# The first norm's squares on one engine, and the MLP's first three products side by side

## The chip, the core and the metric

The program runs on one core of a Trainium2 chip. Its engines work side by side and wait for one another by semaphores: TensorE (PE) multiplies, VectorE (DVE), ScalarE (ACT) and GpSimd (POOL) do elementwise work, and SyncE (SP) hands transfers to the DMA queues. The metric is the device time of one execution in microseconds, as the median of the runs shown.

## The reference

Two transformer blocks in a row, in float32, on 512 tokens of 1024 features. The change touches the first block alone.

```
def rmsnorm(x, g):
    y = x * rsqrt(mean(x * x, axis=-1) + EPS) * g
def first_block(x, ...):
    h = rmsnorm(x, ln1)
    z = h @ w_in                      # split into a pooling, a gated-linear and a forgetting attention mixer
    mix = concat(y_pool, y_gla, y_fox)
    x = x + mix @ w_o
    h = rmsnorm(x, ln2)
    gate, up = split(h @ w_gu)        # 2 x 2816 columns
    x = x + (silu(gate) * up) @ w_down
```

## The kernel before

The activations lie transposed: `x[k]`, for k from 0 to 7, holds features 128k to 128k+127 on the partitions and the 512 tokens along the free axis. Every matrix is split into a high and a low half, so that a product over one row tile k takes three matmuls of 128x512 on TensorE: high weight by high activation (`wh`, `hh`), high by low (`wh`, `hl`), low by high (`wl`, `hh`). A product over all eight row tiles is 24 matmuls into one PSUM bank (`dense`). Banks with the tag `mm` are three, taken in turn.

A weight tile (`weight`) comes by one transfer into `wr` (two buffers), ScalarE makes `wh` of it (line 188) and VectorE or GpSimd makes `wl` (line 189, three buffers of each). The engine for `wl` alternates with the count of tiles. A buffer is free when its last reader has ended.

A norm does not stand before the product that uses it. The activations are scaled by the gain alone and multiplied, and the scale of each token, R = 1/sqrt(mean square), is applied when a product is taken out of PSUM. R itself takes a chain (`rstd`): the squares of the eight row tiles are added up in one tile `ss`; four small matmuls with a column of ones sum `ss` over the partitions (`col_sum`, the rows `tr<-ones,ss`); ScalarE takes the root (`col`), VectorE the reciprocal and its two parts (`part`); eight matmuls spread the result over all partitions (`spread`, rows `tr<-identr,part`); ScalarE copies it to `R`.

The order on TensorE is that in which the code calls it. The other engines' order is set by the tile framework's scheduler when the program is built, and SyncE sends transfers in a fixed order too, each as soon as its buffer is free.

The first norm, in `block1`: for each x[k], as its transfer lands, ScalarE makes `hh` (line 494) and VectorE `hl` (line 495). The four odd squares and their sum are made on GpSimd (lines 502 and 504), the four even ones on ScalarE and added on VectorE (`square_into`, lines 294 and 298), and line 508 adds the two sums. On TensorE, a first small product (`psg`) and, from row tile 3 on, the product `gq` run behind the arriving tiles; then `gk` follows, whose first 15 matmuls stand ahead of `col_sum`.

The MLP's entry: the output projection `w_o` ends with m = 7; for each m VectorE adds the product to x[m] (line 556), ScalarE makes `hh` and VectorE `hl` (lines 192 and 193), and the square goes to `ss`. Then `mlp` multiplies: product 0 (gate of tile 0) over all eight row tiles, product 1 (up of tile 0) with the chain of R inside it, then products 2 and 3 (tile 1), and so on. A gate product is taken out by line 860 (`g<-mm,R`) and an up product by line 864 (`u<-mm,R`).

Of the kernel before, what the change touches and what calls it, by code (L numbers as in the profile page):

```python
# [16 lines left out]
OP = mybir.AluOpType  # L17
# [3 lines left out]
P = 128  # L21
T = 512
D = 1024
KD = D // P
# [60 lines left out]
class Body:  # L85
# [388 lines left out]
    def block1(self, ctx, raw):  # L474
        nc, A, x = self.nc, self.A, self.x
        mp = self.pool(ctx, "mix")
        mix = [tuple(mp.tile([P, T], F32R, name=f"m{c}{k}") for c in "hl") for k in range(4)]
        b = lambda dt=F32: mp.tile([P, T], dt, tag="b", name="b", bufs=NB)

        wg = self.wp.tile([P, 1024], F32R, tag="wh", name="wh", bufs=3)  # L480
        wg3, raw3 = wg.rearrange("p (k m) -> p k m", m=P), raw[:, :512].rearrange("p (k m) -> p k m", m=64)
        self.split(wg3[:, :, :64], wg3[:, :, 64:], raw3)
        rq = self.wp.tile([P, 1024], F32, tag="wr", name="wr", bufs=WR)
        wq = [self.wp.tile([P, 1024], F32R, tag=t, name=t, bufs=3) for t in ("wh", "wl")]
        h = self.acts()
        sums = [self.sums(), self.sums()]
        for k in range(KD):
            for n, at in enumerate((XA, XB)):
                if k == at:
                    cols = slice(n * 512, n * 512 + 512)  # L490
                    nc.sync.dma_start(rq[:, cols], A["w1s"][T1["gq"]][:, cols])
                    self.split(*(w[:, cols] for w in (*wq, rq)))
            nc.sync.dma_start(x[k], A["xT"][k * P:(k + 1) * P, :])
            last = nc.scalar.activation(h[k][0], x[k], AF.Identity, scale=self.gain("ln1", k))
            nc.vector.scalar_tensor_tensor(h[k][1], x[k], self.gain("ln1", k), h[k][0].bitcast(F32),  # L495
                                           op0=OP.mult, op1=OP.subtract)
        self.ident = self.const(self.gp, "ident", [P, P])
        self.identr = self.gp.tile([P, P], F32R, name="identr")
        nc.scalar.activation(self.identr, self.ident, AF.Copy)
        for k in range(1, KD, 2):  # L500
            sq = sums[1] if k == 1 else self.tmp()
            nc.gpsimd.tensor_tensor(sq, x[k], x[k], op=OP.mult)
            if k > 1:
                nc.gpsimd.tensor_tensor(sums[1], sums[1], sq, op=OP.add)
        for k in range(0, KD, 2):
            with self.tc.issue_after(getattr(last, "ins", last)):
                self.square_into(sums[0], x[k], k == 0, eng=nc.vector)
        nc.vector.tensor_tensor(sums[0], sums[0], sums[1], op=OP.add)
        self.identb = self.const(mp, "identb", [P, P], BF16)
        self.causalb = self.const(mp, "causalb", [P, P], BF16)  # L510
        psg = self.bank("mm")
        gen = self.dense(wq, h)
        for k in range(KD):
            for half in (True, False) if k == KD - 1 else (False, True):
                if half:
                    self.mm(psg[:64], wg3[:, k, :64], h[k][1], False, False)
                else:
                    self.mm(psg, wg3[:, k, :], h[k][0], k == 0, k == KD - 1)
            if k >= XL:
                next(gen)  # L520
        psq = self.all(gen)
        gen = self.dense(self.slab("w1s", T1["gk"]), h)
        for _ in range(XS):
            next(gen)
        r = self.rstd(sums[:1], D)
        next(r)
        next(gen)
        next(gen)
        R, Rc = self.all(r)
        psk = self.all(gen)  # L530
        fd = self.dp.tile([8, T], F32, name="fd")
        V = [[], []]
        proj = self.fox_proj(h, R, b)
        with ExitStack() as c:
            self.gla_phase(c, h, R, Rc, mix, mp, b, fd, psg, (psq, psk), V, proj)
        self.share = 1
        with ExitStack() as c:
            xp = self.pool(c, "mix2")
            mix += [tuple(xp.tile([P, T], F32R, name=f"m{c}{k}") for c in "hl") for k in range(4, KD)]
            self.fox_phase(mp, b, mix, V, fd, proj, self.half_zero(xp))  # L540
            self.share = 2
            h2 = self.acts()
            ssum = self.sums()
            for m in range(KD):
                self.all(self.w_o(mix, m, 1))
                self.split_scaled(h2[m][0], h2[m][1], x[m], self.gain("ln2", m))
                self.square_into(ssum, x[m], m == 0, eng=nc.vector if m == KD - 1 else nc.gpsimd)
            self.last = [ssum]
        self.h = h2
# [236 lines left out]
    def fox_phase(self, mp, b, mix, V, fd, proj, klo):  # L786
# [26 lines left out]
        self.attention(begin, after, PFOX, 860, res=RESF, masked=True, norm=NFOX)  # L813
        self.flush()

    def mlp(self, ctx):
        nc, A, x = self.nc, self.A, self.x
        fp = self.pool(ctx, "ff")
        wd = self.pool(ctx, "wd")
        act = [tuple(fp.tile([P, T], F32R, name=f"f{c}{k}") for c in "hl") for k in range(FH)]  # L820
        lng = fp.tile([P, KD], F32, name="lng")
        o, o2 = GAINS["ln_f"][0], GAINS["norm_g"][0]
        nc.vector.tensor_tensor(lng, self.gains[:, o:o + KD], self.gains[:, o2:o2 + KD], op=OP.mult)
        ft = lambda tag: fp.tile([P, T], F32, tag=tag, name=tag, bufs=2)
        self.res = self.dp.tile([T, D], F32, name="res")

        def down(m, half):
            raw = wd.tile([P, FH * P], F32, tag="wd", name="wd", bufs=2)
            nc.sync.dma_start(raw, A["w1d"][half * KD + m])
            hi, lo = (wd.tile([P, FH * P], F32R, tag=t, name=t, bufs=2) for t in ("wdh", "wdl"))  # L830
            self.split(hi, lo, raw)
            return hi, lo

        def turn(m):

            s, o = ft("g"), ft("u")
            nc.scalar.activation(s, x[m], AF.Identity, scale=self.gain("ln_f", m))
            yield
            tr = self.bank("tr")
            for t in range(NT):  # L840
                self.tp(tr[:, t * P:(t + 1) * P], s[:, t * P:(t + 1) * P])
            nc.scalar.activation(o, tr, AF.Copy)
            nc.sync.dma_start(self.res[:, m * P:(m + 1) * P].rearrange("(t p) c -> p t c", p=P),
                              o.rearrange("p (t c) -> p t c", c=P))

        turns = []
        for half in range(2):
            for k in range(FH):
                m = half * FH + k
                ps = self.all(self.dense(self.slab("w1gu", 2 * m), self.h))  # L850
                gen = self.dense(self.slab("w1gu", 2 * m + 1), self.h)
                if m == 0:
                    r = self.rstd(self.last, D)
                    next(gen)
                    next(r)
                    for _ in range(3):
                        next(gen)
                    R = self.all(r)[0]
                g = ft("g")
                nc.vector.tensor_tensor(g, ps, R, op=OP.mult)  # L860
                nc.scalar.activation(g, g, AF.Silu)
                ps = self.all(gen)
                u = ft("u")
                nc.vector.tensor_tensor(u, ps, R, op=OP.mult)  # L864
                nc.vector.tensor_tensor(u, u, g, op=OP.mult)
                self.split(act[k][0], act[k][1], u)
            for m in range(KD):
                ps = self.all(self.dense(down(m, half), act, kt=FH))
                nc.vector.tensor_tensor(x[m], ps, x[m], op=OP.add)  # L869
                if half == 1:  # L870
                    if m == 0:
                        h = self.acts()
                        s1, s2 = self.sums(), self.sums()
                    self.split_scaled(h[m][0], h[m][1], x[m], lng[:, m:m + 1])
                    eng = nc.vector if m == KD - 1 else nc.gpsimd
                    self.square_into(s1, x[m], m == 0, eng=eng)
                    self.square_into(s2, x[m], m == 0, scale=self.gain("ln_f", m), eng=eng)
                    for g in turns:
                        self.all(g)
                    turns = [turn(m)]  # L880
                    next(turns[0])
        self.s1, self.s2 = [s1], [s2]
        self.h, self.turns = h, turns
# [584 lines left out]
```

## Time and profile before

| what | value |
|---|---|
| runs (us) | 1092.42, 1092.99, 1090.87; median 1092.42 |
| the profiled execution | 1092.89 us, of which the span of the records is 1090.3 us |
| granted TensorE clock, mean over the span | 0.985 of full |
| busy over the span | PE 97%, weight loads 80%, DVE 62%, ACT 50%, POOL 35% |
| chain that ended last, by engine | PE 75%, DVE 17%, ACT 3%, DMA 2%, issue 2% |

Times in rows are microseconds from the start of the span. A row with a count xN covers N instructions in a row, and its busy time is theirs together. A bracket at the end of a row is the engine's idle time ahead of it and what ended that. Neighbouring matmuls overlap in the records, so the pace of TensorE is read from the distance of their starts.

### The profile page before, as it was taken

The numbers are of one execution on the slowest core, as the hardware profiler recorded it, in microseconds if no ns is written. First come the engines' busy times: TensorE is split into PE (matmuls) and PEld (weight loads), VectorE is DVE, ScalarE is ACT, GpSimd is POOL, SyncE is SP. The second block draws the span as 40 slices with busy tenths as digits, with TensorE's granted clock in tenths as the row PEclk, the third lists the DMA queues.
The fourth block names the chain that finished last, engine by engine and source line by source line (L and its number), as shares of the span: only waits on it lengthen the run. The fifth ranks groups of instructions, "written<-read, shape, count | busy, mean of one in ns | idle before, by whom it ended". The sixth has DMA issues, their size and how long they took to land.

```text
span 1090.3 us, 14058 instructions
## 1 busy us (share of the span) xinstructions
PE 1053.8 (97%) x5264; PEld 871.0 (80%) x5264; DVE 675.2 (62%) x1137; ACT 543.2 (50%) x950; POOL 377.6 (35%) x221
## 2 busy tenths in 40 slices
PE   8999999998999999999999998989899999999997
PEld 4888877787888888888888787768787898888786
DVE  7654488885454432445444268899996566888652
ACT  5653578654232221223235465655655566678233
POOL 5233322133232300223123254433334346654454
PEclk9999999998999999999999999899999999999999
DMA  6322132252323323232323144232222323335842
GB/s 202 102 78 78 56 101 67 69 183 72 102 95 98 96 81 106 87 114 80 106 85 118 29 131 151 70 106 90 89 87 97 110 67 121 112 87 175 281 152 77
DMA packets 41690, 114.81 MB, mean 105 GB/s; under 512 B 4952, under 2 KB 9448, under 8 KB 41624
## 3 DMA queue, kind: packets, MB, share of 16 engines
q1 hardware_dynamic: 38536, 107.62, 30.6%
q10 hardware_dynamic: 2448, 4.22, 1.0%
q0 software_dynamic: 640, 2.10, 0.5%
q8 instruction: 41, 0.67, 0.2%
q14 instruction: 25, 0.20, 0.1%
HBM read 103.40 MB, written 13.14 MB: 107 GB/s over the span
## 4 chain that ended last, share of the span: by engine, by line
PE 75%; DVE 17%; ACT 3%; DMA 2%; issue 2%; SPq 0%; DVEq 0%; ACTq 0%
PE mm L151 64%; PE sc L151 4%; PE pv L151 3%; PE tr L151 2%; DVE score L1005 2%; PE tr L158 2%; DVE m L1004 2%; DVE kst L189 1%; DVE pl L387 1%; DMA wr<-in_w2uq_r 1%; DVE hl L193 1%; DVE b L311 1%; DVE qk L189 1%; DVE b L374 1%; DVE s L369 1%
## 5 line engine op out<-in xcount | busy, mean ns | idle before, releaser
L189 POOL TENSOR_TENSOR wl<-wr,wh 128x1024 fp32r<-128x1024 f32 (+2 forms) x107 | 263.3, 2461 | 560.9 <-ACT wh L188 547.9
L151 PE MATMUL mm<-hh,wh 128*128 128x512 f32 (+2 forms) x808 | 327.0, 405 | 2.4 <-DVE z L1076 1.6
L151 PE MATMUL mm<-hl,wh 128*128 128x512 f32 (+3 forms) x808 | 318.1, 394 | 5.9 <-DVE hl L495 3.5
L151 PE MATMUL mm<-hh,wl 128*128 128x512 f32 (+1 forms) x800 | 314.8, 394 | 0.0
L188 ACT ACTIVATE wh<-wr 128x1024 fp32r<-128x1024 f32 (+2 forms) x142 | 146.8, 1034 | 225.7 <-PE mm L151 186.4
L151 PEld LDWEIGHTS mm<-hl,wh 128*128 128x128 f32 (+2 forms) x808 | 153.5, 190 | 36.7 <-DVE hl L495 6.2
L151 PEld LDWEIGHTS mm<-hh,wh 128*128 128x128 f32 (+1 forms) x808 | 154.1, 191 | 34.5 <-DVE z L1076 2.0
L151 PEld LDWEIGHTS mm<-hh,wl 128*128 128x128 f32 (+1 forms) x800 | 151.5, 189 | 32.8
L151 PE MATMUL mm<-fh,wdh 128*128 128x512 f32 x176 | 70.1, 398 | 0.0
L151 PE MATMUL mm<-fl,wdh 128*128 128x512 f32 x176 | 69.6, 395 | 0.0
L151 PE MATMUL mm<-fh,wdl 128*128 128x512 f32 x176 | 69.6, 395 | 0.0
L864 DVE TENSOR_TENSOR u<-mm,R 128x512 f32<-128x512 f32 x22 | 15.2, 692 | 72.2 <-PE mm L151 72.2
L188 ACT ACTIVATE wdh<-wd 128x1408 fp32r<-128x1408 f32 x16 | 22.1, 1381 | 74.4 <-PE mm L151 70.5
L869 DVE TENSOR_TENSOR x<-mm,x 128x512 f32<-128x512 f32 x16 | 11.1, 692 | 74.2 <-PE mm L151 74.2
L189 DVE TENSOR_TENSOR fl<-u,fh 128x512 fp32r<-128x512 f32 x22 | 45.0, 2044 | 15.4 <-ACT fh L188 15.4
L387 DVE TENSOR_TENSOR pl<-tr,ph 128x128 fp32r<-128x128 f32 (+1 forms) x96 | 46.0, 484 | 11.2 <-ACT ph L386 10.2
L298 POOL TENSOR_TENSOR ss<-ss,t 128x512 f32<-128x512 f32 x21 | 30.8, 1479 | 51.9 <-ACT t L297 51.9
L371 ACT ACTIVATE s<-s,m 128x128 f32<-128x128 f32 (+1 forms) x64 | 35.8, 559 | 25.3 <-DVE m L369 24.9
L189 DVE TENSOR_TENSOR wl<-wr,wh 128x1024 fp32r<-128x1024 f32 (+1 forms) x34 | 42.4, 1248 | 8.0 <-ACT wh L188 7.8
L151 PE MATMUL mm<-wh,hh 128*128 128x256 f32 x160 | 46.5, 290 | 0.0
L151 PE MATMUL mm<-wl,hh 128*128 128x256 f32 x160 | 45.3, 283 | 0.0
L151 PE MATMUL mm<-wh,hl 128*128 128x256 f32 x160 | 45.2, 283 | 0.0
(345 smaller groups left out, 2022.9 us busy)
## 6 DMA issues: line engine op xcount, KB each, us to landing
wr<-in_w1gu SPq DMA_DIRECT2D x44, 512.0 KB, 3.5
wr<-in_w2s SPq DMA_DIRECT2D x39, 512.0 KB, 3.5
wd<-in_w1d SPq DMA_DIRECT2D x16, 704.0 KB, 4.3
wr<-in_w1s SPq DMA_DIRECT2D x15, 512.0 KB, 3.5
wr<-in_w1o SPq DMA_DIRECT2D x8, 512.0 KB, 3.5
wr<-in_w2o SPq DMA_DIRECT2D x8, 512.0 KB, 3.8
shear<-gd SPq DMA_DIRECT2D x1, 2560.0 KB
x<-in_xT SPq DMA_DIRECT2D x8, 256.0 KB, 5.8
```

The lines of the kernel that those rows point to most:

```text
L151: self.nc.tensor.matmul(out, l, r, start=start, stop=stop)
L158: self.nc.tensor.transpose(out, src, self.ident if ident is None else ident)
L188: self.nc.scalar.activation(hi, src, AF.Copy)
L189: (eng or self.nc.vector).tensor_tensor(lo, src, hi.bitcast(F32), op=OP.subtract)
L193: self.nc.vector.scalar_tensor_tensor(lo, src, scale, hi.bitcast(F32), op0=OP.mult, op1=OP.subtract)
L298: (eng or nc.gpsimd).tensor_tensor(ssum, ssum, sq, op=OP.add)
L371: nc.scalar.activation(s[:, :n], s[:, :n], AF.Exp, scale=-1.0, bias=m[:, 0:1], accum_out=m[:, 1:2])
L387: nc.vector.tensor_tensor(lo, trv, hi.bitcast(F32), op=OP.subtract)
L864: nc.vector.tensor_tensor(u, ps, R, op=OP.mult)
L869: nc.vector.tensor_tensor(x[m], ps, x[m], op=OP.add)
L1004: nc.vector.max(out=m8, in_=s)
L1005: nc.vector.match_replace(s, m8, s, -3.4e38)
```

## The change

In `block1`, all eight squares are made on ScalarE and seven are added on VectorE; GpSimd has no part in them, and there is one sum tile instead of two. In `mlp`, the first three products are started side by side in three banks: row tiles 0 to 5 of products 0, 1 and 2, then `col_sum`, then row tiles 6 and 7 of products 0 and 1, then `spread`, then row tiles 6 and 7 of product 2. The number of matmuls stays.

```diff
-        sums = [self.sums(), self.sums()]
+        ssum = self.sums()
...
-        for k in range(1, KD, 2):
-            sq = sums[1] if k == 1 else self.tmp()
-            nc.gpsimd.tensor_tensor(sq, x[k], x[k], op=OP.mult)
-            if k > 1:
-                nc.gpsimd.tensor_tensor(sums[1], sums[1], sq, op=OP.add)
-        for k in range(0, KD, 2):
+        for k in range(KD):
             with self.tc.issue_after(getattr(last, "ins", last)):
-                self.square_into(sums[0], x[k], k == 0, eng=nc.vector)
-        nc.vector.tensor_tensor(sums[0], sums[0], sums[1], op=OP.add)
+                self.square_into(ssum, x[k], k == 0, eng=nc.vector)
...
-        r = self.rstd(sums[:1], D)
+        r = self.rstd([ssum], D)
...
+    def entry(self):
+
+        n, late = 3, KD - 2
+        w = [self.weight(self.A["w1gu"][i]) for i in range(n)]
+        self.first = [self.bank("mm") for _ in range(n)]
+
+        def part(i, ks):
+            for k in ks:
+                (hi, lo), (ah, al), c = w[i], self.h[k], slice(k * P, (k + 1) * P)
+                self.mm(self.first[i], hi[:, c], ah, k == 0, False)
+                self.mm(self.first[i], hi[:, c], al, False, False)
+                self.mm(self.first[i], lo[:, c], ah, False, k == KD - 1)
+
+        r = self.rstd(self.last, D)
+        for i in range(n):
+            part(i, range(late))
+        next(r)
+        part(0, range(late, KD))
+        part(1, range(late, KD))
+        self.R2 = self.all(r)[0]
+        part(2, range(late, KD))
...
-                ps = self.all(self.dense(self.slab("w1gu", 2 * m), self.h))
-                gen = self.dense(self.slab("w1gu", 2 * m + 1), self.h)
                 if m == 0:
-                    r = self.rstd(self.last, D)
-                    next(gen)
-                    next(r)
-                    for _ in range(3):
-                        next(gen)
-                    R = self.all(r)[0]
+                    self.entry()
+                ps = self.first.pop(0) if self.first else self.all(self.dense(self.slab("w1gu", 2 * m), self.h))
+                gen = None if self.first else self.dense(self.slab("w1gu", 2 * m + 1), self.h)
```

The scheduler's order on VectorE at the first norm, from the last `hl` on, before (`ss` is the sum, `t` a square, the first `wl` that of `gk`, the second that of the second `gv` tile, `b` the small product taken from PSUM):

```order
L495 SCALAR_TENSOR_TENSOR hl7_150<-x7_117,gains_82,hh7_149 128x512
L298 TENSOR_TENSOR ss_151<-ss_151,t_198 128x512
L189 TENSOR_TENSOR wl_257<-wr_254,wh_256 128x1024
L298 TENSOR_TENSOR ss_151<-ss_151,t_201 128x512
L587 TENSOR_TENSOR b_339<-mm_212,t_340 64x512
L298 TENSOR_TENSOR ss_151<-ss_151,t_204 128x512
L508 TENSOR_TENSOR ss_151<-ss_151,ss_152 128x512
L189 TENSOR_TENSOR wl_370<-wr_367,wh_369 128x1024
L262 RECIPROCAL col_281<-col_281 128x4
```

And now:

```order
L495 SCALAR_TENSOR_TENSOR hl7_150<-x7_117,gains_82,hh7_149 128x512
L298 TENSOR_TENSOR ss_151<-ss_151,t_187 128x512
L298 TENSOR_TENSOR ss_151<-ss_151,t_190 128x512
L298 TENSOR_TENSOR ss_151<-ss_151,t_193 128x512
L189 TENSOR_TENSOR wl_257<-wr_254,wh_256 128x1024
L298 TENSOR_TENSOR ss_151<-ss_151,t_196 128x512
L298 TENSOR_TENSOR ss_151<-ss_151,t_199 128x512
L298 TENSOR_TENSOR ss_151<-ss_151,t_202 128x512
L298 TENSOR_TENSOR ss_151<-ss_151,t_205 128x512
L581 TENSOR_TENSOR b_339<-mm_212,t_340 64x512
L189 TENSOR_TENSOR wl_370<-wr_367,wh_369 128x1024
L262 RECIPROCAL col_281<-col_281 128x4
```

Seven adds to `ss` stand there instead of three, and the add of line 508 is gone (later lines are numbered six lower in the changed file). On ScalarE, at the same place, from the first square on, the order is now this (`wh_256` is `gk`, `wh_363` the first `gv` tile, `wh_369` the second):

```order
L294 ACTIVATE ss_151<-x0_110 128x512
L297 ACTIVATE t_187<-x1_111 128x512
L297 ACTIVATE t_190<-x2_112 128x512
L499 ACTIVATE identr_184<-c_ident_182 128x128
L297 ACTIVATE t_193<-x3_113 128x512
L188 ACTIVATE wh_256<-wr_254 128x1024
L297 ACTIVATE t_196<-x4_114 128x512
L297 ACTIVATE t_199<-x5_115 128x512
L297 ACTIVATE t_202<-x6_116 128x512
L188 ACTIVATE wh_363<-wr_361 128x1024
L297 ACTIVATE t_205<-x7_117 128x512
L580 ACTIVATE t_340<-mm_212 64x512
```

Before, only x2, x4 and x6 had a `t` there, and the first `gv` tile stood behind all of them; now the last square stands behind it. On TensorE at the MLP's entry the piece that carries the sum is the turn from the first to the last row tiles, which is now (`mm_2581`, `mm_2582`, `mm_2583` are products 0, 1 and 2):

```order
L151 MATMUL mm_2583<-hh5_2349,wh_2577 128x512
L151 MATMUL mm_2583<-hl5_2350,wh_2577 128x512
L151 MATMUL mm_2583<-hh5_2349,wl_2578 128x512
L151 MATMUL tr_2638<-ones_84,ss_2355 128x1 x4
L151 MATMUL mm_2581<-hh6_2351,wh_2565 128x512
L151 MATMUL mm_2581<-hl6_2352,wh_2565 128x512
L151 MATMUL mm_2581<-hh6_2351,wl_2566 128x512
L151 MATMUL mm_2581<-hh7_2353,wh_2565 128x512
L151 MATMUL mm_2581<-hl7_2354,wh_2565 128x512
L151 MATMUL mm_2581<-hh7_2353,wl_2566 128x512
```

Before, the matmuls of `hh6` and `hl6` in product 0 stood right behind those of `hl5` in the same product, with no others between. On ScalarE the `wh` of the fourth tile stood ahead of the root `col`; now the fourth and the fifth stand between `col` and `R`. On VectorE the `wl` of the fourth tile moved from ahead of the reciprocal to behind `part`. The order of transfers on SyncE is the same, and GpSimd has lost the seven instructions of the first norm and nothing else.

## Rows read from the trace of the kernel before

**Rows 1.** Whom TensorE waited for, whole span: total, times, longest.
```profile
PE mm L151 <- DVE hl L495: 3.5, 4, 2.1
PE mm L151 <- DVE hl L193: 2.3, 2, 2.2
```

**Rows 2.** Timeline of TensorE from 6 to 27 us: start, busy, instruction.
```profile
12.14 0.45 PE L151 MATMUL mm<-hl,wh 128*64 128x512 f32 x1 [2.11 <-DVE hl L495]
...
18.41 0.44 PE L151 MATMUL mm<-hl,wh 128*64 128x512 f32 x1 [0.33 <-DVE hl L495]
...
25.99 0.95 PE L151 MATMUL tr<-ones,ss 128*128 128x1 f32 x8
```

**Rows 3.** Timeline of VectorE from 0 to 60 us.
```profile
8.21 0.75 DVE L495 SCALAR_TENSOR_TENSOR hl<-x,gains,hh 128x512 fp32r<-128x512 f32 x1 [0.62 <-ACT hh L494]
...
10.33 3.20 DVE L495 SCALAR_TENSOR_TENSOR hl<-x,gains,hh 128x512 fp32r<-128x512 f32 x2
...
14.90 4.12 DVE L495 SCALAR_TENSOR_TENSOR hl<-x,gains,hh 128x512 fp32r<-128x512 f32 x3
...
19.54 1.21 DVE L189 TENSOR_TENSOR wl<-wr,wh 128x1024 fp32r<-128x1024 f32 x1
...
22.71 2.71 DVE L508 TENSOR_TENSOR ss<-ss 128x512 f32<-128x512 f32 x1
```

**Rows 4.** Timeline of GpSimd from 0 to 60 us.
```profile
14.39 3.41 POOL L504 TENSOR_TENSOR ss<-ss,t 128x512 f32<-128x512 f32 x2
22.32 2.54 POOL L189 TENSOR_TENSOR wl<-wr,wh 128x1024 fp32r<-128x1024 f32 x1 [4.52 <-ACT wh L188]
```

**Rows 5.** Timeline of ScalarE from 0 to 60 us.
```profile
10.79 2.09 ACT L494 ACTIVATE hh<-x,gains 128x512 fp32r<-128x512 f32 x3
12.79 0.61 ACT L294 ACTIVATE ss<-x 128x512 f32<-128x512 f32 x1
...
24.19 1.06 ACT L188 ACTIVATE wh<-wr 128x1024 fp32r<-128x1024 f32 x1 [1.95 <-DMA wr<-in_w1gv]
```

**Rows 6.** Timeline of SyncE's queue from 0 to 60 us.
```profile
15.00 6.11 SPq L197 DMA_DIRECT2D wr<-in_w1gv  x2
```

**Rows 7.** Chain that ended last, by line: 18 to 146, then 263 to 640 us.
```profile
by line: PE mm L151 79.4%; PE tr L151 7.1%; PE sc L151 6.8%; PE pv L151 5.0%; DVE hl L495 1.3%; PE tr L158 1.2%; DVE b L369 0.3%; issue 0.1%; DVEq L369 0.0%
by line: PE mm L151 98.3%; PE tr L158 1.0%; PE tr L151 0.8%
```

**Rows 8.** Timeline of TensorE from 245 to 278 us.
```profile
246.29 0.39 PE L151 MATMUL mm<-hh,wh 128*128 128x512 f32 x1
...
254.95 0.50 PE L151 MATMUL mm<-hl,wh 128*128 128x512 f32 x1 [2.16 <-DVE hl L193]
...
256.87 1.70 PE L151 MATMUL tr<-ones,ss 128*128 128x1 f32 x8
...
262.36 1.00 PE L151 MATMUL tr<-identr,part 128*128 128x128 f32 x8
...
266.00 0.39 PE L151 MATMUL mm<-hh,wh 128*128 128x512 f32 x1
...
276.88 0.39 PE L151 MATMUL mm<-hh,wh 128*128 128x512 f32 x1
```

**Rows 9.** Busy time by stretch: length, PE, PEld, DVE, ACT, POOL, granted clock, DMA.
```profile
258.00:260.00 2.00, 2.00 (x7) 1.71 (x8) 0.51 (x3) 0.26 (x1) 0.00 (x0) 0.50 0.49 164
```

**Rows 10.** Timeline of VectorE from 225 to 300 us.
```profile
252.28 2.62 DVE L193 SCALAR_TENSOR_TENSOR hl<-x,gains,hh 128x512 fp32r<-128x512 f32 x1 [0.79 <-ACT hh L192]
254.82 0.68 DVE L298 TENSOR_TENSOR ss<-ss,t 128x512 f32<-128x512 f32 x1
...
264.02 0.69 DVE L860 TENSOR_TENSOR g<-mm,R 128x512 f32<-128x512 f32 x1 [4.54 <-ACT R L280]
```

**Rows 11.** Timeline of GpSimd from 220 to 300 us.
```profile
252.00 2.35 POOL L189 TENSOR_TENSOR wl<-wr,wh 128x1024 fp32r<-128x1024 f32 x1
```

**Rows 12.** Timeline of ScalarE from 215 to 290 us.
```profile
263.39 0.60 ACT L280 ACTIVATE R<-tr 128x512 f32<-128x512 f32 x1 [4.52 <-PE tr L151]
```

More of the change, by code (lines that the diff above doesn't have):

```diff
@@ L849, in mlp @@
                 m = half * FH + k
-                ps = self.all(self.dense(self.slab("w1gu", 2 * m), self.h))
-                gen = self.dense(self.slab("w1gu", 2 * m + 1), self.h)
                 if m == 0:
-                    r = self.rstd(self.last, D)
-                    next(gen)
-                    next(r)
-                    for _ in range(3):
-                        next(gen)
-                    R = self.all(r)[0]
+                    self.entry()
+                ps = self.first.pop(0) if self.first else self.all(self.dense(self.slab("w1gu", 2 * m), self.h))
+                gen = None if self.first else self.dense(self.slab("w1gu", 2 * m + 1), self.h)
                 g = ft("g")
-                nc.vector.tensor_tensor(g, ps, R, op=OP.mult)
+                nc.vector.tensor_tensor(g, ps, self.R2, op=OP.mult)
                 nc.scalar.activation(g, g, AF.Silu)
-                ps = self.all(gen)
+                ps = self.first.pop(0) if gen is None else self.all(gen)
                 u = ft("u")
-                nc.vector.tensor_tensor(u, ps, R, op=OP.mult)
+                nc.vector.tensor_tensor(u, ps, self.R2, op=OP.mult)
                 nc.vector.tensor_tensor(u, u, g, op=OP.mult)
```

## The prediction

> **What bounds the kernel now.** I read the list of TensorE's waits first, then the chain that ended last by stretch, then the timelines of each engine at the two places of the change, with the granted clock beside them. TensorE is the engine that matters. From 18 to 146 us and from 263 to 640 us nearly every step of the chain is its own work [rows 7], so a microsecond taken from it ahead of these stretches should come out at the end. Two entries in its list of waits are the low halves of the two norms: 3.5 us for `hl` of line 495 and 2.3 us for `hl` of line 193 [rows 1].
>
> At the first norm VectorE is late because of GpSimd. An `hl` that runs alone takes 0.75 us; two of them together then take 3.20 and three take 4.12, 1.4 to 1.6 us each [rows 3], while GpSimd makes its squares and sums, the last of which end at 14.39 + 3.41 = 17.80 us [rows 4]. ScalarE has all its `hh` done at 10.79 + 2.09 = 12.88 us [rows 5], but the last `hl` ends at 14.90 + 4.12 = 19.02 us, six microseconds later. TensorE stands for 2.11 us ahead of 12.14 us, and still waits for an `hl` at 18.41 us [rows 2].
>
> At the MLP's entry the last `hl` is held up too: it takes 2.62 us from 252.28 us, and ends 0.55 us behind the 2.35 us of GpSimd from 252.00 us [rows 10, 11]. Product 0 needs it straight away, so TensorE waits 2.16 us [rows 8]. After that wait the granted clock is 0.50 of full, the lower level of 1.2 GHz, for the stretch from 258 to 260 us [rows 9]. So the wait is paid once as idleness and once more as slow matmuls.
>
> **The entry's price, worked out.** Product 0 starts at 246.29 us and product 4 at 276.88 us [rows 8]: 30.59 us for four products, one `col_sum` and one `spread`. At full clock 48 matmuls go from 266.00 to 276.88 us, 0.2267 us each [rows 8]. Four products are 96 matmuls, 21.76 us; `col_sum` at full clock is 0.95 us [rows 2] and `spread` 1.00 us [rows 8]. That is 23.71 us if nothing waits, **6.9 us less** than now.
>
> Does anything wait in the new order? The first 54 matmuls use only row tiles 0 to 5 and fill 246.29 to 258.53 us. `ss` is done at 254.82 + 0.68 = 255.50 us and the last `hl` at 254.90 us [rows 10], ahead of `col_sum` at 258.53 us and of their own use from about 259.5 us. Of the weights, product 2's `wl` is the tight one: it ends at 252.00 + 2.35 = 254.35 us on GpSimd [rows 11], and is first read by the 39th matmul, at 246.29 + 38 x 0.2267 = 254.90 us. It is 0.55 us to spare, the smallest margin I find. With no wait, nothing asks for the lower clock.
>
> What is late next is product 3. Its bank is that of product 0, which `g<-mm,R` must take out first. Now, from the start of `spread` at 262.36 us to the end of that multiply at 264.02 + 0.69 = 264.71 us are 2.35 us, with the copy to R at 263.39 us between [rows 8, 10, 12]. In the new order TensorE has `spread` (1.00) and six matmuls of product 2 (1.36) to do in that time, 2.36 us: they match, and I put 0.1 us for the wait. The weights of product 3 start later than now, since product 0 keeps its `wh` buffer until its last row tiles end, at 258.53 + 0.95 + 1.36 = 260.84 us. Then come 1.06 us of `wh` [rows 5] and 1.21 us of `wl` [rows 3], to 263.1 us, ahead of 264.6 us. The fifth `wh` now stands ahead of the copy to R on ScalarE. It needs product 1's buffer, free at 262.2 us, so it ends near 263.3 us, when `spread` ends too. That hides it; without this cover each microsecond of it would delay R and product 3 by as much. The entry's term is **-6.8 us**. Its bounds: -6.9, and +0 if the same waits come back elsewhere.
>
> **The first norm's price.** Without GpSimd, an `hl` takes 0.75 us [rows 3], and the last follows the last `hh` at 12.88 us: some 13.7 us instead of 19.0. The third `hl` waits for half a `wl` (I take 0.6 us, half of 1.21 [rows 3]) and ends near 8.96 + 0.6 + 0.75 = 10.3 us instead of 12.1. From there 48 matmuls stand ahead of `col_sum` (33 to the end of `gq`, 15 of `gk`): 10.9 us at full clock, so TensorE would come to `col_sum` at 21.2 us. Now it is there at 25.99 us [rows 2]. The upper bound of this term is thus 4.8 us.
>
> But `ss` must be ready. ScalarE has four more squares, 4 x 0.61 = 2.4 us [rows 5], and the last stands behind the `wh` of the first `gv` tile. Counted from 12.79 us: four squares, the small `identr` (0.3, an estimate from its quarter size), one `wh`, three squares, one `wh`. With starts 0.52 to 0.61 us apart, that `wh` ends at 18.7 to 19.5 us and the last square at 19.2 to 20.1. The tile's transfer is handed over at 15.00 us at the latest [rows 6]. The next tile's hand-over ends at 15.00 + 6.11 = 21.11 us, and its `wh` waits for the landing and starts at 24.19 us [rows 5, 6], about 3.4 us from one to the other. So the first lands by 18.4 us, and earlier if its buffer, released by VectorE's faster half `wl`, lets it go earlier.
>
> When that `wh` ends, GpSimd takes the tile's `wl`, 2.54 us [rows 4], to 21.2 or 22.0 us, and the last add falls in it. Beside the same kind of `wl` today, an add that started at 22.71 us took 2.71 us and ended at 25.42, 0.56 us after GpSimd's 22.32 + 2.54 = 24.86 us [rows 3, 4]. So I let the last add end 0.56 us after GpSimd, at 21.8 to 22.6 us, and `col_sum` with it: 3.4 to 4.1 us sooner than now. Behind the add, VectorE still has `b` and a `wl` of 1.21 us [rows 3] ahead of the reciprocal, as before. The root is there about a microsecond after `col_sum`, so the parts can come 0.2 us late for `spread`. My value is **-3.7 us**, between -4.8 and 0.
>
> Here the Trainium skill has a rule, in "SBUF — State Buffer", section "SBUF: two separate sides": a VectorE instruction with two SBUF inputs and a GpSimd instruction exclude each other, whichever starts first holds the shared ports for its whole length, and the other stands. By it the last add ends behind the `wl`, and the sum is as above. If the two only slowed each other down, as the 1.4 to 1.6 us per `hl` [rows 3] could also be read, the add would end by 21.5 us, and the term would be up to -4.8 us. The add that ends 0.56 us after GpSimd [rows 3, 4] and the `hl` that ends 0.55 us after it [rows 10, 11] speak for the rule.
>
> **What is free.** The seven instructions that GpSimd loses lie off the chain, apart from what they do to VectorE. The three extra adds, 0.68 us each [rows 10], fall in the six microseconds that VectorE gains.
>
> **The sum.** 1092.89 us of the profiled execution (span 1090.3 and 2.6 around it) less 6.8 and 3.7 is 1082.4 us. The median of the runs is 0.5 us below that execution, so I say **1081.9 us**, 1.0% less. A difference under 0.2%, about 2 us, can't be told from none here.
>
> **The rivals.** (1) No exclusion: the last add is in time and the norm gives 4.8; 1080.8 us. For it speaks the 1.4 us `hl`, against it the two late ends. Chance 0.12. (2) The norm's gain is lost on the way to the MLP: the attention between 146 and 228 us is set by several engines, and the list of chain shares shows TensorE alone only to 146 us [rows 7]. But nothing there is fixed to an absolute time, so a shift should pass through. 1092.4 - 6.8 = 1085.6 us; chance 0.14. (3) The entry still waits, because product 2's `wl` has just 0.55 us to spare or product 3's bank comes late. If half of the 6.8 is left over, 1085.3 us; chance 0.10. (4) No change beyond the noise: both gains are given back, 1092 us; chance 0.04. (5) Slower: on ScalarE the last square stands behind a `wh` that waits for a transfer, and the square, the sum, R and all products behind it wait along, microsecond for microsecond. It decides from a landing 10.5 us later than the 18.4 us above, near 29 us; at 34 us the time would be 1097 us. The 3.4 us landing [rows 5, 6] speaks against it. Chance 0.04.
>
> **How the numbers follow.** My forecast, within 1.5 us, has 0.56. With (1) to (3) below 1086.3 us, the range of 1080.0 to 1086.3 us holds a little over 8 in 10, since (1) and (3) can pass its ends. Faster 0.90, same 0.05, slower 0.05.
>
> **What would show it.** Right: the `hl` of the first norm at 0.75 us and the last ended before 15 us; `col_sum` at 22 us; no wait of TensorE for line 193 and no stretch at 0.50 clock at the MLP's entry; 23.8 us from the start of product 0 to that of product 4. Wrong: `col_sum` still near 25 us, a wait for `ss` or for product 3's bank of a microsecond or more, or a stretch from `col_sum` to the MLP that is longer than now by what the norm gained.

## The result, and the profile after

The changed kernel takes 1081.36 us, the median of four runs (1080.86 to 1083.48), beside 1092.70 us for the kernel before on the same chip: a ratio of 0.9899, with a 95% interval of 0.9877 to 0.9922. That is 11 us less; 1081.9 us was forecast, in a range of 1080.0 to 1086.3. The profiled execution took 1081.27 us, with a span of 1079.5 us at a mean clock of 0.990. Two more executions of the changed kernel and one more of the kernel before were profiled later.

The list of whom TensorE waited for, in the changed kernel (total, times, longest):

```profile
PE tr L151 <- DVE ss L298: 1.1, 1, 1.1
...
PE mm L151 <- DVE hl L495: 0.5, 2, 0.3
```

Of the two entries of [rows 1], that of line 193 is gone and that of line 495 fell from 3.5 to 0.5 us. A new one of 1.1 us stands for the first norm's `ss`. VectorE at the first norm:

```profile
8.70 1.44 DVE L495 SCALAR_TENSOR_TENSOR hl<-x,gains,hh 128x512 fp32r<-128x512 f32 x2
...
10.74 2.12 DVE L495 SCALAR_TENSOR_TENSOR hl<-x,gains,hh 128x512 fp32r<-128x512 f32 x3
...
16.48 5.22 DVE L298 TENSOR_TENSOR ss<-ss,t 128x512 f32<-128x512 f32 x4
```

Five `hl` take 0.7 us each, where [rows 3] had 1.4 to 1.6, and the last ends at 12.86 us, six microseconds sooner. But the last four adds take 5.22 us, not four times 0.68. VectorE there, in a narrower stretch:

```profile
18.07 2.84 DVE L298 TENSOR_TENSOR ss<-ss,t 128x512 f32<-128x512 f32 x1
```

GpSimd in the same stretch:

```profile
17.97 2.40 POOL L189 TENSOR_TENSOR wl<-wr,wh 128x1024 fp32r<-128x1024 f32 x1 [14.45 <-DVE ss L298]
```

An add that started just behind GpSimd's `wl` stood until 20.91 us, 0.54 us after the `wl` ended, and the last add came behind it, to 21.70 us. TensorE over the same time:

```profile
21.76 1.05 PE L151 MATMUL tr<-ones,ss 128*128 128x1 f32 x8 [1.05 <-DVE ss L298]
...
23.61 0.63 PE L151 MATMUL mm<-hh,wh 128*128 128x512 f32 x1
24.04 0.63 PE L151 MATMUL mm<-hl,wh 128*128 128x512 f32 x1
...
24.89 1.80 PE L151 MATMUL tr<-identr,part 128*128 128x128 f32 x8
```

Busy time by stretch there and at the MLP's entry, with the columns of [rows 9] (the third number from the end is the granted clock):

```profile
24.00:26.00 2.00, 2.00 (x9) 1.77 (x8) 0.00 (x0) 0.00 (x0) 0.00 (x0) 0.50 0.71 229
...
258.00:260.00 2.00, 2.00 (x13) 1.67 (x11) 0.63 (x1) 1.35 (x2) 0.00 (x0) 1.00 0.00 0
```

`col_sum` starts 4.23 us sooner than in [rows 2], but the matmuls behind it stand 0.43 us apart instead of 0.23: the clock is at its lower level there, and `spread` takes 1.80 us. That price is paid in this execution alone of the three, as the experiments show. Ahead of `col_sum` the first norm gained clock. In the kernel before, the wait of 2.11 us that ended at 12.14 us [rows 2] was followed by half clock too, a stretch that the prediction does not name. The kernel before:

```profile
14.00:16.00 2.00, 1.98 (x5) 0.99 (x3) 2.00 (x2) 1.07 (x2) 2.00 (x2) 0.50 0.37 83
```

Now neither that wait nor that stretch is left:

```profile
14.00:16.00 2.00, 2.00 (x10) 1.65 (x9) 1.90 (x3) 2.00 (x4) 0.00 (x0) 1.00 0.75 243
```

At the MLP's entry, 258 to 260 us had 0.50 in [rows 9] and has 1.00 now. TensorE at the entry:

```profile
243.77 0.39 PE L151 MATMUL mm<-hh,wh 128*128 128x512 f32 x1
...
256.01 0.95 PE L151 MATMUL tr<-ones,ss 128*128 128x1 f32 x8
...
259.69 1.00 PE L151 MATMUL tr<-identr,part 128*128 128x128 f32 x8
...
262.11 0.50 PE L151 MATMUL mm<-hh,wh 128*128 128x512 f32 x1
...
267.70 0.39 PE L151 MATMUL mm<-hh,wh 128*128 128x512 f32 x1
```

The first and last rows are the starts of products 0 and 4: 23.93 us, where [rows 8] gave 30.59. The last `hl` of the entry on VectorE:

```profile
249.75 2.68 DVE L193 SCALAR_TENSOR_TENSOR hl<-x,gains,hh 128x512 fp32r<-128x512 f32 x1 [0.79 <-ACT hh L192]
```

And GpSimd beside it:

```profile
249.48 2.40 POOL L189 TENSOR_TENSOR wl<-wr,wh 128x1024 fp32r<-128x1024 f32 x1
```

It still takes 2.68 us beside GpSimd, as in [rows 10, 11]; but it is done at 252.43 us and read after 257 us. The change did not shorten this work, it moved its reader behind other work.

### The profile page after: what moved, and what is told of

Same layout as the page of the kernel before. It is cut to its first block, busy times and chain, and to the rows that moved or that the text cites. A ratio compares the mean times of both kernels' runs of the same rounds, so it can differ in the third digit from the quotient of the medians.

```text
span 1079.5 us, 14066 instructions
## 1 busy us (share of the span) xinstructions
PE 1048.9 (97%) x5264; PEld 868.8 (80%) x5264; DVE 671.8 (62%) x1140; ACT 545.5 (51%) x954; POOL 366.8 (34%) x214
## 4 chain that ended last, share of the span: by engine, by line
PE 79%; DVE 14%; ACT 2%; issue 2%; DMA 1%; SPq 0%; DVEq 0%; ACTq 0%
PE mm L151 67%; PE sc L151 4%; PE pv L151 3%; PE tr L151 2%; PE tr L158 2%; DVE kst L189 2%; DVE score L1016 1%; DVE m L1015 1%; DVE pl L387 1%; DVE b L311 1%; DVE b L374 1%; DVE qk L189 1%; DVE s L369 1%; DVE s L1069 1%; DVE b L369 1%
## 5 line engine op out<-in xcount | busy, mean ns | idle before, releaser
L880 DVE TENSOR_TENSOR x<-mm,x 128x512 f32<-128x512 f32 x16 | 11.1, 692 | 73.3 <-PE mm L151 73.3
L189 DVE TENSOR_TENSOR fl<-u,fh 128x512 fp32r<-128x512 f32 x22 | 42.1, 1914 | 14.7 <-ACT fh L188 14.7
L386 ACT ACTIVATE ph<-tr 128x128 fp32r<-128x128 f32 (+1 forms) x96 | 40.5, 427 | 9.4 <-PE tr L158 8.7
```

The costliest lines, as they stand in the source:

```text
L189: (eng or self.nc.vector).tensor_tensor(lo, src, hi.bitcast(F32), op=OP.subtract)
L386: nc.scalar.activation(hi, trv, AF.Copy)
```

## The experiments

**Theory:** VectorE's instructions with two SBUF inputs stand still while GpSimd works. The first norm gains because GpSimd leaves it, the entry because row tile 7 is read later. A long wait of TensorE also costs a stretch at half clock. **Rivals:** the entry's waits have another cause; the norm's gain is lost on its way to the MLP; the gain comes from the second block.

All profiled executions by four marks, in us: the start of the first norm's copy to R, of the MLP's product 0, of the last `wdl` (the low half of the last down weights, near the first block's end), and of the first output transfer. Ratios are to the kernel before on the same chip.

| kernel | R | product 0 | last `wdl` | out | ratio (95%) |
|---|---|---|---|---|---|
| before | 29.33 | 246.29 | 605.4 | 1078.4 | |
| before, again | 28.99 | 245.98 | 605.1 | 1077.6 | |
| norm alone | 25.08 | 242.17 | 602.5 | 1069.3 | 0.9963 (0.9946 to 0.998) |
| entry alone | 29.39 | 246.43 | 598.9 | 1070.1 | 0.9918 (0.9898 to 0.9939) |
| last `hl` unblocked | 29.17 | 246.06 | 600.8 | 1072.1 | 0.9956 (0.9942 to 0.9969) |
| changed | 26.73 | 243.77 | 596.3 | 1067.4 | 0.9899 (0.9877 to 0.9922) |
| changed, again | 25.45 | 242.35 | 594.8 | 1066.3 | 0.9897 (0.9884 to 0.9911) |
| changed, third | 25.52 | 242.53 | 595.0 | 1068.3 | |
| two products | 25.59 | 242.61 | 597.7 | 1070.3 | 0.9897 (0.9871 to 0.9924) |
| square first | 25.34 | 242.35 | 594.8 | 1067.8 | 0.9882 (0.986 to 0.9905) |
| square first, again | 24.64 | 241.65 | 594.1 | 1066.0 | 0.9891 (0.9875 to 0.9907) |
| sum later | 25.31 | 245.52 | 598.0 | 1070.7 | 0.994 (0.9925 to 0.9954) |
| sum earlier | 26.61 | 244.97 | 597.4 | 1070.4 | 0.9925 (0.991 to 0.994) |

**The two parts apart.** First the norm's edit alone, with the MLP as before:

```diff
...
-                self.square_into(sums[0], x[k], k == 0, eng=nc.vector)
-        nc.vector.tensor_tensor(sums[0], sums[0], sums[1], op=OP.add)
+                self.square_into(ssum, x[k], k == 0, eng=nc.vector)
...
```

> Only the first norm's edit; the MLP's entry as before. My theory: the products behind the first norm start some 2.5 us sooner (what the changed kernel shows at the copy to R: 26.7 against 29.3 us), that shift passes through the attention unchanged to the MLP's entry (product 0 near 243.8 us), and the entry itself keeps its 30.6 us; total 2.5 us faster, 1089.9 against 1092.4, or up to 4 us if the clock at the second block's start falls well too. Rival that the norm's gain is lost on the way to the MLP: product 0 near 246.3 us and the total within 1 us of before. If the x tiles land 0.8 us sooner because GpSimd doesn't square, the sixth hh starts near 10.0 us here and near 10.8 us in the run that has only the entry's edit.

Then the MLP's edit alone, as the changed kernel with the norm of before:

```diff
-        ssum = self.sums()
+        sums = [self.sums(), self.sums()]
...
-        for k in range(KD):
+        for k in range(1, KD, 2):
+            sq = sums[1] if k == 1 else self.tmp()
+            nc.gpsimd.tensor_tensor(sq, x[k], x[k], op=OP.mult)
...
```

> Only the MLP's entry; the first norm as before. My theory: product 0 starts at 246.3 us as before and product 4 23.8 us later; 6.8 us faster, near 1085.6, and whatever the clock at the second block's start adds or takes, at most 2 us either way. Rival that the two edits need each other (the entry waits again when it stands at another place in time): a wait of TensorE for line 193 or for ss at the entry, and less than 5 us.

From R to product 0 the two kernels take 217.09 and 217.04 us by the table, as the kernel before does (216.96): a gain at the norm passes through whole, and the rival that loses it on the way is out. From product 0 to the last `wdl` the entry alone takes 352.5 us, the kernel before 359.1, the norm alone 360.3: 6.6 us belong to the entry, and the norm alone gives 4.1 us at product 0. The timed runs give the two parts 4.0 us (2.2 to 5.9) and 9.0 us (6.7 to 11.1); the second is more than the 6.8 us that were expected, and together they are more than the 11 us of the change. The intervals are too wide to say more, so the sizes of the parts rest on the traces.

R also moves with the landing of x, since ScalarE makes each `hh` as its tile lands. The sixth `hh` starts at 9.89 us in the norm alone and at 10.14 us in the entry alone. That GpSimd's squares hold the tiles up by 0.8 us is not borne out: over all thirteen executions the sixth `hh` starts at 10.14 to 10.79 us with these squares and at 9.82 to 10.91 without. From that start to R the kernel before takes 18.54 and 18.56 us and the norm alone 15.19.

In the norm alone the entry's wait is as before; its TensorE there:

```profile
250.82 0.80 PE L151 MATMUL mm<-hl,wh 128*128 128x512 f32 x1 [2.17 <-DVE hl L193]
...
258.67 1.80 PE L151 MATMUL tr<-identr,part 128*128 128x128 f32 x8
```

Its busy time by stretch and clock:

```profile
254.00:256.00 2.00, 2.00 (x7) 1.81 (x8) 0.51 (x3) 0.28 (x2) 0.00 (x0) 0.50 0.45 119
```

**Why the last `hl` is late.** The kernel before, with product 2's `wl` made by VectorE behind that `hl`, so that GpSimd has nothing to do there. The order of the products stays.

```diff
...
+        def third():
+            with self.tc.issue_after(lo_last):
+                return self.weight(A["w1gu"][2], pool=False)
...
-                ps = self.all(self.dense(self.slab("w1gu", 2 * m), self.h))
+                ps = self.all(self.dense(third if m == 1 else self.slab("w1gu", 2 * m), self.h))
```

> The kernel before with one thing changed: the lower part of product 2's weights is worked out by VectorE behind the last lower part of the MLP's input, not by GpSimd beside it. The order of the products stays as it was. Theory (VectorE's lower part stands still while GpSimd works on that weight tile): the last lower part takes about 0.75 us, TensorE's wait of 2.16 us for it shrinks to 0.2 to 0.4 us, and product 0 to product 4 takes between 28.7 us (the wait alone is gone) and 25 us (the half clock behind it is gone too); time 2 to 5.5 us below the kernel before. Rival (the last lower part is late for another reason, its input or its queue): the wait stays above 1.5 us and the time within 1 us of before.

VectorE in this kernel:

```profile
252.04 0.75 DVE L193 SCALAR_TENSOR_TENSOR hl<-x,gains,hh 128x512 fp32r<-128x512 f32 x1 [0.79 <-ACT hh L192]
252.71 1.22 DVE L189 TENSOR_TENSOR wl<-wr,wh 128x1024 fp32r<-128x1024 f32 x1
```

TensorE:

```profile
252.85 0.49 PE L151 MATMUL mm<-hl,wh 128*128 128x512 f32 x1 [0.29 <-DVE hl L193]
254.68 1.02 PE L151 MATMUL tr<-ones,ss 128*128 128x1 f32 x8 [0.41 <-DVE ss L298]
```

Busy time by stretch and clock:

```profile
258.00:260.00 2.00, 2.00 (x13) 1.75 (x13) 0.60 (x1) 1.21 (x2) 0.00 (x0) 1.00 0.36 147
```

The `hl` takes 0.75 us instead of 2.62 [rows 10], the wait is 0.29 us instead of 2.16 [rows 8], and the clock is full where [rows 9] had half. By the table, product 0 to the last `wdl` falls by 4.4 us: 1.9 us are the wait, the other 2.5 what followed it. The entry of the change gives 2.2 us more; this kernel keeps small waits, of which the two of 0.29 and 0.41 us stand above. GpSimd's weight tile made the last `hl` late.

**How many products side by side.** The changed kernel with two instead of three.

```diff
-        n, late = 3, KD - 2
+        n, late = 2, KD - 2
...
-        part(2, range(late, KD))
```

> The changed kernel with two products side by side at the MLP's entry instead of three. col_sum comes after 36 matmuls, 8.2 us after product 0 starts; in the changed kernel ss is ready 9.3 us after that start and the last hl 8.7 us after it. My theory: TensorE waits about 1.1 us for ss, and a wait of that length is followed by a stretch at half clock as behind the first norm's col_sum (1.6 us lost there); 1 to 4 us slower than the changed kernel, 1082.5 to 1085.5. Rival that two products are cover enough: no wait over 0.3 us, within 1 us of the changed kernel.

Its TensorE:

```profile
252.03 1.02 PE L151 MATMUL tr<-ones,ss 128*128 128x1 f32 x8 [1.10 <-DVE ss L298]
```

Its busy time by stretch and clock:

```profile
254.00:256.00 2.00, 2.00 (x7) 1.57 (x6) 0.53 (x1) 1.06 (x1) 0.00 (x0) 0.54 0.00 0
```

With 36 matmuls as cover the sum is late by 1.10 us, and the clock falls behind it. Product 0 to the last `wdl` is 355.1 us, 2.6 us more than with three. The timed runs don't show the 1 to 4 us that were expected: 0.9897 beside 0.9899 and 0.9897, with intervals that overlap. That three are worth 2.6 us rests on the traces.

**The last add behind GpSimd.** The changed kernel with the last square of the first norm ahead of the first `gv` tile's `wh`, from which GpSimd's `wl` starts.

```diff
...
-            w = [self.weight(A["w1gv"][a]) for a in range(2)]
+            with self.tc.issue_after(getattr(sq_last, "ins", sq_last)):
+                w = [self.weight(A["w1gv"][0])]
+            w.append(self.weight(A["w1gv"][1]))
```

> The changed kernel, with the last square of the first norm ahead of the wh of the first gv tile on ScalarE: one swap. Theory that GpSimd's wl holds the last add up until it ends: now the add comes before that wl, ss is done near 19 us, col_sum starts at 20.6 us without a wait instead of 21.8 us, and with no wait there is no stretch at half clock behind it; the copy to R near 24 us instead of 26.7, and 2 to 3 us faster than the changed kernel, near 1078.7. Rival that the add was late for another cause (ScalarE's square or VectorE's own queue): col_sum stays within 0.4 us of 21.8. Rival that the half clock behind col_sum is not from the wait: the wait goes and the stretch at 0.50 stays, 1.2 us gained only.

VectorE in the first of the two runs:

```profile
17.36 3.08 DVE L298 TENSOR_TENSOR ss<-ss,t 128x512 f32<-128x512 f32 x4
```

TensorE in it:

```profile
21.46 0.95 PE L151 MATMUL tr<-ones,ss 128*128 128x1 f32 x8
```

Four adds take 3.08 us, not 5.22, and TensorE no longer waits for them. The copy to R was expected near 24 us and starts at 25.34: x landed late, with the sixth `hh` at 10.91 us. A second run stands beside the changed kernel itself.

> The changed kernel with the first norm's last square ahead of the upper part of the first weight tile, again, now on one chip with the changed kernel itself. The column sum loses its wait of about 1 us for the last add, and the half clock behind it has nothing to start from: the row's copy ends 3.9 to 4.3 us before that of the kernel before, product 0 likewise. Where the changed kernel shows the half clock it is 1 to 1.6 us slower than this one; where it does not, the two lie within 0.5 us. Rival (the square ahead only moves the lateness to the weights): products of the first weight tile start later and the two are equal or this one is slower.

The changed kernel itself, run again on the same chip:

> The changed kernel once more, beside the others of this call. Both theories of the 1.6 us that its profiled execution lost between the first norm's column sum (-4.2 us) and the normalised row (-2.6 us) see a column sum that waits about 1.0 to 1.4 us for VectorE's last add. If the half clock behind it is a consequence of that wait, the products that follow stand 0.43 us apart again and the row's copy ends at 26 to 27 us. If it comes and goes from one execution to the next, as the same wait without a half clock in the two kernels before suggests, the clock is full this time and the copy ends at 24.8 to 25.6 us. Product 0 to product 4 of the MLP: 23.8 us again either way. Time 10.5 to 12.5 us below the kernel before.

And a third execution of it:

> The changed kernel a third time, for one more look at whether the half clock follows the first norm's column sum: it did in one of two executions so far, behind waits of 1.05 and 0.97 us. Full clock: the row's copy at 25.2 to 25.7 us and product 0 at 242.1 to 242.6 us. Half clock: 26.4 to 27 us and 243.5 to 244 us. Product 0 to product 4 at 23.9 us in both cases.

Both executions show full clock at the first norm, behind a wait about as long as that of the first execution. TensorE, in the second, with ScalarE's sixth `hh` ahead of it:

```profile
10.33 2.15 ACT L494 ACTIVATE hh<-x,gains 128x512 fp32r<-128x512 f32 x3
...
22.02 1.05 PE L151 MATMUL tr<-ones,ss 128*128 128x1 f32 x8 [0.97 <-DVE ss L298]
...
24.41 1.00 PE L151 MATMUL tr<-identr,part 128*128 128x128 f32 x8
```

And in the third:

```profile
22.10 1.05 PE L151 MATMUL tr<-ones,ss 128*128 128x1 f32 x8 [1.24 <-DVE ss L298]
```

So the 1.3 us by which R was later in the first execution (26.73 against 25.45 and 25.52) come and go. Counted from the sixth `hh`, R comes after 16.75 us in the first execution, 15.12 us in the second and third, and 14.43 and 14.53 us with the square first. The square first is thus worth 0.6 to 0.7 us, and half clock cost 1.6. Product 0 comes at 241.65 us at best, 0.7 us ahead of the changed kernel, of which 0.2 us are x. The ratios are the lowest measured, but their intervals overlap those of the changed kernel, so it is not shown to be faster.

**The column sum moved.** The changed kernel, three matmuls later, with the last three ahead of `spread`:

```diff
-XS = 5
+XS = 6
...
         next(r)
         next(gen)
-        next(gen)
-        R, Rc = self.all(r)
         psk = self.all(gen)
+        R, Rc = self.all(r)
```

> The changed kernel with the first norm's column sum three matmuls later: 18 of the second product's matmuls ahead of it, not 15, and the last three ahead of the spread, not behind it. The sum of squares is ready when it was. Theory (TensorE's idle time here is lost one for one, since it has work of its own up to 146 us): the wait ahead of the column sum falls from about 1.0 to 0.3 us, its start stays at 21.7 to 22.2 us, no half clock follows, and product 0 of the MLP starts at 241.5 to 241.9 us, 0.5 to 0.8 us before the changed kernel at full clock (242.35). Rival (what counts is when the normalising row is there): product 0 stays at 242.2 to 242.6 us. Time 0 to 1 us below the changed kernel either way.

And six matmuls earlier (`XS = 3`):

> The changed kernel with the first norm's column sum six matmuls earlier (9 ahead of it instead of 15). Theory (idle time lost one for one): the wait ahead of the column sum grows by 1.4 us to 2.3 to 2.7 us, and product 0 starts 1.4 us later at full clock, 243.5 to 244.0 us. If a longer wait brings the half clock on, as the 2.16 us wait at the MLP's entry did in both executions of the kernel before, the matmuls behind it stand 0.43 us apart, the row's copy ends 1.3 to 2 us later than 25.45 us, and product 0 starts at 244.8 to 246 us. Rival (what counts is when the row is there): product 0 stays at 242.2 to 242.6 us at full clock.

The first of them missed both expectations. Its wait for `ss` did shrink to 0.28 us, but from R to product 0 it took 220.2 us instead of 217.0. Its VectorE:

```profile
25.92 2.44 DVE L581 TENSOR_TENSOR ga<-b,R 16x512 f32<-16x512 f32 x1 [2.27 <-ACT R L280]
```

Its GpSimd:

```profile
25.48 2.34 POOL L189 TENSOR_TENSOR wl<-wr,wh 128x1024 fp32r<-128x1024 f32 x1 [4.59 <-ACT wh L188]
```

Its TensorE:

```profile
28.42 1.12 PE L151 MATMUL tr<-ga,c_wau 16*128 16x512 f32 x2 [2.78 <-DVE ga L581]
```

Its busy time by stretch and clock:

```profile
30.00:32.00 2.00, 2.00 (x12) 2.00 (x11) 1.44 (x3) 1.97 (x3) 0.00 (x0) 0.50 0.33 135
```

ScalarE now makes a `wh` ahead of the copy to R, and so GpSimd's `wl` starts just before VectorE's `ga`, which took 0.68 us in the changed kernel and takes 2.44 here. TensorE waits for it and then runs at half clock. The same exclusion came back in another place, and it cost 3 us.

With the earlier sum TensorE waits 2.54 us, as its timeline shows:

```profile
21.61 1.28 PE L151 MATMUL tr<-ones,ss 128*128 128x1 f32 x8 [2.54 <-DVE ss L298]
```

The half clock follows, as expected; busy time by stretch:

```profile
24.00:26.00 2.00, 2.00 (x9) 1.61 (x8) 0.00 (x0) 0.00 (x0) 0.00 (x0) 0.58 0.79 252
```

R is 1.1 us later, a little less than the 1.3 to 2 us expected, and from R to product 0 it takes 218.4 us, 1.4 more: that is the six matmuls of 0.2267 us which now stand behind the sum instead of in the wait. Idle time of TensorE is lost one for one here.

**Where the rest came from.** The first two profiles differ by 10.9 us at the first output transfer, but by 9.1 us at the last `wdl`. A second execution of the kernel before:

> The kernel before once more, for one look at the second block. About 1.5 us of the gain in the profiled executions lies at the second norm, where the granted clock was 0.55 over 10 us before and 0.95 after, and the change does not touch that place. If the half clock there belongs to the kernel before, it comes again at 680 to 690 us (0.5 to 0.65 over 10 us). If it differs between executions, it may show 0.75 or more. At the MLP's entry of the first block: the same waits of about 0.2, 0.6 and 2.2 us for the lower parts, and 30 to 31 us from product 0 to product 4.

In it TensorE waits 2.17 us at the entry again and has the half clock behind; at 680 to 690 us the clock is 0.59, as it was 0.55 in the first execution. Its TensorE at the entry:

```profile
254.63 0.80 PE L151 MATMUL mm<-hl,wh 128*128 128x512 f32 x1 [2.17 <-DVE hl L193]
```

From the last `wdl` to the first output transfer the kernel before takes 473.0 and 472.5 us and the changed kernel 471.1, 471.5 and 473.3 us. So the second block is a matter of the execution within some 2 us, and the rival that the gain comes from there is out as an explanation of ten microseconds. The norm alone took only 466.8 us in it, in an execution of 1083.07 us that was the fastest of twelve (median 1089.20). By the traces, a meeting of VectorE and GpSimd stands behind most of this. In the other twelve profiled executions a VectorE instruction of an attention in the second block starts behind a `wl` of GpSimd and takes 2.38 us, and TensorE waits 3.6 us for what follows it. VectorE, GpSimd and TensorE of the kernel before:

```profile
781.70 2.38 DVE L1007 TENSOR_SCALAR score<-score 128x384 f32<-128x384 f32 x1
...
781.32 2.54 POOL L189 TENSOR_TENSOR wl<-wr,wh 128x1024 fp32r<-128x1024 f32 x1 [2.76 <-ACT wh L188]
...
784.96 1.12 PE L158 MATMUL tr<-c_ident,s 128*128 128x128 f32 x4 [3.61 <-ACT s L376]
```

In the norm alone it comes ahead of the `wl`:

```profile
777.57 0.36 DVE L1001 TENSOR_SCALAR score<-score 128x384 f32<-128x384 f32 x1
...
778.32 2.40 POOL L189 TENSOR_TENSOR wl<-wr,wh 128x1024 fp32r<-128x1024 f32 x1 [2.19 <-ACT wh L188]
```

TensorE waits 0.55 us there and keeps full clock, where the kernel before has 0.63 and 0.52 from 784 to 788 us. By the starts of ScalarE's rows on either side, this saves 4.4 us against this execution of the kernel before. Ahead of it VectorE's `kst` and GpSimd's `qk` had started within 0.04 us of each other: they took 0.69 and 1.85 us, where the kernel before has 1.79 and 1.28. Why VectorE came first this once is not shown.

## Why the prediction was right

- **The entry, -6.8 us.** Measured -6.66 (23.93 instead of 30.59), and 352.4 to 352.5 us from product 0 to the last `wdl` in every kernel with the three products, against 359.1. `col_sum` stands at 256.01 us, which is 243.77 plus 54 x 0.2267. The wait for product 3's bank was 0.16 us (0.39 us between the starts at 261.72 and 262.11 us, not 0.23), where 0.1 was allowed. The sum had two sizes wrong that nearly cancel: right behind `col_sum`, `spread` and that wait a row tile takes 0.74 to 0.80 us instead of 0.68, and from start to start `col_sum` and `spread` take 0.81 and 0.84 us, not their busy times of 0.95 and 1.00. The margin of product 2's `wl`, 0.55 us by the forecast, was 0.5 (251.88 against the 39th matmul at 252.38 us). The rival that the entry still waits is out.
- **The norm, -3.7 us.** R is there at 25.45 and 25.52 us at full clock, against 29.33 and 28.99: -3.7 by the means, of which some 0.25 us are x landing sooner; counted from the sixth `hh` it is -3.4. In the execution that was profiled first it was -2.6, because of the half clock behind the new wait, which the forecast did not reckon with. The `hl` took 0.7 us each, and the last ended before 15 us. The rival that is slower than before is out: the last square waited for no transfer. (The 3.4 us from hand-over to landing that the forecast set against it run from the start of the hand-over at 20.78 us; from its end at 21.11 us it is 3.1.)
- **The last add behind the `wl`.** It was to end 0.56 us after GpSimd. In the second execution the last add ends at 19.27 + 2.70 = 21.97 us, 0.55 us after it. In the first and third it is the add before that which stands, and the last comes 0.8 us behind. `col_sum` at 21.76, 22.02 and 22.10 us agrees with the forecast's 22, but in these two by luck: ScalarE was early, so the `wl` ended at 20.37 and 20.70 us, not at 21.2 to 22.0, and one more add than was foreseen stood behind it, which made up for that. The rival with no exclusion is out: the adds took 5.22 us beside GpSimd and 3.08 us without it. The Trainium skill's rule ("SBUF — State Buffer", section "SBUF: two separate sides"), by which the one of the two engines that starts first keeps the shared ports for its whole instruction and the other stands, holds here. The run with the unblocked `hl` (2.62 to 0.75 us) takes such a meeting away, and the later sum (0.68 to 2.44 us) makes one.
- **One sign was badly set.** A wait for `ss` of a microsecond was named as a sign that the forecast is wrong. It came (0.97 to 1.24 us), and the account held all the same: the working itself had TensorE there at 21.2 us and the sum at 21.8 to 22.6, which is a wait of 0.6 to 1.4 us. TensorE was there at 20.7 to 21.1 us.
- **The sum.** The two terms make 10.5 us; at the last `wdl` the full-clock executions are 10.1 to 10.6 us ahead of those of the kernel before. The timed difference of 11 us holds this within its interval (8.5 to 13.4 us). That the median came within 0.5 us of the forecast is luck: the second block alone differs by 2 us between executions.

## What to carry to other kernels

Before an elementwise instruction on VectorE is called short, look at what GpSimd does in the same microsecond: here a weight tile on GpSimd added 1.8 to 2.2 us to the VectorE instructions shown that started behind it, and moving one engine's order by a step moved the meeting to another victim. Where such a delay can't be removed, put other products between the late tile and its reader; the entry lost its 2.16 us wait though its last `hl` takes as long as ever. When a wait of TensorE is priced, look at the clock behind it too: here taking away 1.9 us of waiting gave 4.4 us.

## What the runs showed of the hardware

- At the two places, waits of TensorE of 2.16, 2.17, 2.17, 2.54 and 2.78 us were each followed by a stretch at 0.50 to 0.58 clock, and so were the waits for an `hl` of line 495 in the four executions with GpSimd's squares (2.11, 2.17, 2.21 and 2.40 us). Of six waits between 0.97 and 1.41 us two were: one of three at the same place of the changed kernel, and that of 1.10 us with two products. The Trainium skill ("TensorE: Matmul & The Clock Gate", section "Part 1: The HAM clock gate") says that the chip's watch on activity runs on freely and doesn't start with the kernel; two outcomes of one wait would fit that, but no run here shows that it is the cause.
- The exclusion has a tail: VectorE instructions that take 0.68 to 0.75 us alone ended 0.54 to 0.56 us after GpSimd's, and the one of 0.36 us ended 0.22 us after it (781.70 + 2.38 against 781.32 + 2.54 us). An instruction that stood still needs nearly all of its own time behind GpSimd. The last of these has one tile as input, not two, and stood all the same.
- It works the other way as well. In the second execution of the changed kernel GpSimd's `wl` is recorded with 2.93 us, where it took 2.40 in the first; its record begins beside an add that ran from 18.48 for 0.69 us, and it ended 2.25 us after that add:

```profile
18.49 2.93 POOL L189 TENSOR_TENSOR wl<-wr,wh 128x1024 fp32r<-128x1024 f32 x1 [14.98 <-ACT wh L188]
```
